# Half of the feed-forward's first product in four blocks by seven products for eight, with the second product's units moved to the odd blocks

## The chip, the cores and the metric

One core of a Trainium2 chip runs the whole kernel. The metric is the time on the device in microseconds (us); a lower one is better. TensorE (PE) multiplies matrices into PSUM, VectorE (DVE) and ScalarE (ACT) work element by element, GpSimd (POOL) issues some of the DMAs and SyncE (SP) the others.

## The reference, cut to what matters

The reference is a decoder trunk of two layers over 256 tokens of width 2048, all in float32. Each layer has an attention and then a feed-forward part; only the second is touched:

```python
FFN_HIDDEN = 5632

def _swiglu(h, w_in, w_out):
    g, u = jnp.split(h @ w_in, [FFN_HIDDEN], axis=-1)
    return (jax.nn.silu(g) * u) @ w_out

def reference(x, positions, norm_gains, ...):
    for i in range(DEPTH):
        ...
        x = x + _rmsnorm(y, g[1])
        y = _swiglu(_rmsnorm(x, g[2]), ffn_w_in[i], ffn_w_out[i])
        x = x + _rmsnorm(y, g[3])
    return x
```

`_rmsnorm` divides a token's row by its root mean square and multiplies by a gain for each column. The kernel puts the gains on the transposed tokens, and multiplies by the token's factor (`rstd`) only behind the first product, as a scale for each row.

## The kernel before, in words

**Split numbers.** A float32 matrix product is made of three passes in the reduced format fp32r. Each operand is split into a high part (ScalarE rounds it, line 104) and a low part (VectorE subtracts, line 105), and `mm3` (line 95) adds high x high, high x low and low x high in PSUM. So each piece of weights that is loaded costs two ScalarE casts and two VectorE subtractions of 128x1024 (`split_weight`, halves of the piece), and each use of it with 128 tokens costs 4 x 3 = 12 matmuls with 512 columns. Below, such a group of 12 is called a product. The split halves go to six buffers each (`whi`, `wlo`), which is room for three pieces.

**Blocks.** The 5632 hidden columns are handled in 11 blocks of 512 (`ffn`, line 458). `block_in` (line 463) makes a block's gate and up sums: for m = 0 (gate) and m = 1 (up), for four pieces pc of the 2048 rows (512 rows each) it loads and splits a piece of `win` and multiplies it with both halves of the tokens (t = 0, 1): 16 products in four PSUM buffers (`mm`). The `yield` behind each piece hands over to the caller, which puts other work there. At the end ScalarE makes the silu of the gate sums (line 485), VectorE multiplies it with the up sums (line 487), and TensorE transposes the hidden values (line 492).

**Units.** The second product (hidden x `wout`) is done for pairs of blocks: hidden values of two token halves and two blocks, times the weights of two blocks and two groups of 512 output columns. `unit` (line 555) does this with seven products in place of eight (Strassen's scheme in Winograd's form). The token operands are sums that `pair_operands` (line 503) makes in `first` and `second`, as the two blocks of a pair end: three VectorE operations at the end of the first block, eight at the end of the second. The weight sums are made in three raw buffers (`wr`): `t` starts as B11, then gets B12 by an accumulating DMA from GpSimd (line 571), B22 by a VectorE add (line 568), and B21 by another; `b22` gets B12 by a second accumulating DMA. Each product reads one of these, split anew, and `gather` (lines 579 to 584) adds its sum to `y`. Two of the sums stay in PSUM and are accumulated on.

```python
factor = ("t", "t", "t", "b22", "b22", "b21", "t")
prepare(0)
now = split(w["t"])
yield
for k, left in enumerate(("A11", "S1", "S2", "S4", "S3", "A12", "A22")):
```

**The loop.** From block 2 on, each block has one unit of the pair before beside its own 16 products: the first two column groups in the even block, the other two in the odd one. At each `yield` of `block_in` the loop takes one step of the unit, so a unit's product stands behind each input piece until the seven are done. Block 10 has no partner: its pair's last unit and two plain column groups run beside it.

**What sets the order.** The order in which the code issues work is a priority. A planner at build time puts each engine's instructions in order: of those whose inputs and buffers are ready by its own reckoning, the earliest in the code goes first. A buffer of a pool is given to whoever comes when one is free. The order that comes out is fixed, and on the chip each engine follows it and waits where an input isn't there.

The names that the change touches: `block_in`, `x_piece` (line 326), `unit` with `prepare`, `gather` and `product`, the loop over `blk`, and `x`, the residual stream in SBUF (16 KB a partition), which is not read from the middle of block 0 to the end of block 10.

## Time and profile before

| what | us |
|---|---|
| median of 3 runs | 2108.28 (2108.18 to 2108.62) |
| the profiled execution, its own time | 2108.73 |
| its span (first to last instruction) | 2107.0 |
| mean granted clock of TensorE, share of full speed | 0.995 |
| feed-forward loop of layer 0: block 2 to block 9, cut at the transposes | 500.46 to 1009.76 |
| the same in layer 1 | 1482.60 to 1991.01 |

The profile is of one execution. A line such as "L105" is a line of the kernel's source; "wlo<-w,whi" names the tile that is written and those that are read. Busy time of TensorE overlaps from matmul to matmul, since their ends are modelled: what one costs is seen from start to start. Idle time is put down to what ended it.

### The profile page before, as it was taken

To read this page: it belongs to the slowest core of one execution; us is meant where nothing else is said; L and a number is where in the kernel's file an instruction comes from. 1 tells how busy PE (TensorE), PEld (TensorE's weight loads), DVE (VectorE), ACT (ScalarE), POOL (GpSimd) and SP (SyncE) were. 2 spreads that over 40 slices of the span, in tenths; PEclk is the share of its full clock that TensorE was granted. 3 is DMA by queue.
4 is the path that set the end of the run, shared out by engine and by line. 5 is a ranking of instruction groups with operands and counts; after the bars stand their busy time and mean duration, and the time that the engine had idled before them with its cause. 6 is when DMAs were issued, how large, how long until landed. Compare 5 with 4: busy or idle time off the path is not lost.

```text
span 2107.0 us, 26201 instructions
## 1 busy us (share of the span) xinstructions
PE 2075.4 (98%) x10372; PEld 1770.4 (84%) x10372; DVE 1466.5 (70%) x1697; ACT 1100.6 (52%) x1427; POOL 74.3 (4%) x119
## 2 busy tenths in 40 slices
PE   8999999999999999999998999999999999999997
PEld 7999998788888888888888898878888888888886
DVE  6655555756767778777767776575768768778766
ACT  6444444544555545555445554454555555546543
POOL 0000000000000000000000100000000000000000
PEclk9999999999999999999999999999999999999999
DMA  7554556465676666676644533555566776666663
GB/s 266 200 173 167 163 178 229 153 217 154 226 240 206 206 187 228 220 250 203 198 163 159 209 121 137 182 216 181 197 194 212 239 240 201 213 185 222 217 200 105
DMA packets 62044, 413.85 MB, mean 196 GB/s; under 512 B 7392, under 2 KB 7648, under 8 KB 13920
## 3 DMA queue, kind: packets, MB, share of 16 engines
q1 hardware_dynamic: 56736, 374.42, 49.0%
q0 software_dynamic: 5184, 37.75, 9.8%
q8 instruction: 81, 1.33, 0.3%
q14 instruction: 43, 0.35, 0.0%
HBM read 410.05 MB, written 2.10 MB: 196 GB/s over the span
## 4 chain that ended last, share of the span: by engine, by line
PE 87%; issue 5%; DVE 4%; DMA 2%; ACT 1%; POOL 0%; SPq 0%; POOLq 0%; DVEq 0%; ACTq 0%
PE ps L99 23%; PE ps L101 23%; PE ps L100 23%; PE wp L100 5%; PE wp L101 4%; PE wp L99 4%; DMA wr<-in_wout 2%; DVE wlo L105 2%; DVE x L259 1%; PE pt L492 1%; PE pt L111 1%; PE ps_s L906 0%; PE ps_s L386 0%; PE ps_s L907 0%; PE po L425 0%
## 5 line engine op out<-in xcount | busy, mean ns | idle before, releaser
L105 DVE TENSOR_TENSOR wlo<-w,whi 128x1024 fp32r<-128x1024 f32 (+2 forms) x598 | 716.5, 1205 | 309.5 <-ACT whi L104 297.6
L104 ACT CAST whi<-w 128x1024 fp32r<-128x1024 f32 (+2 forms) x598 | 613.8, 1036 | 452.7 <-PE ps L101 248.5
L99 PE MATMUL ps<-whi,xTh 128*128 128x512 f32 (+2 forms) x1632 | 627.5, 389 | 3.0 <-ACT xTh L104 1.5
L100 PE MATMUL ps<-wlo,xTh 128*128 128x512 f32 (+2 forms) x1632 | 629.4, 387 | 0.0
L101 PE MATMUL ps<-whi,xTl 128*128 128x512 f32 (+2 forms) x1632 | 628.7, 387 | 0.4 <-DVE xTl L105 0.4
L105 DVE TENSOR_TENSOR wlo<-wr,whi 128x1024 fp32r<-128x1024 f32 x252 | 303.2, 1222 | 212.7 <-ACT whi L104 205.9
L104 ACT CAST whi<-wr 128x1024 fp32r<-128x1024 f32 x252 | 261.8, 1050 | 361.0 <-PE ps L101 241.1
L99 PEld LDWEIGHTS ps<-whi,xTh 128*128 128x128 f32 x1632 | 308.1, 189 | 63.9 <-ACT xTh L104 4.4
L101 PEld LDWEIGHTS ps<-whi,xTl 128*128 128x128 f32 x1632 | 307.9, 189 | 60.7 <-DVE xTl L105 0.6
L100 PEld LDWEIGHTS ps<-wlo,xTh 128*128 128x128 f32 x1632 | 308.1, 189 | 59.7 <-DVE wlo L105 0.4
L99 PE MATMUL ps<-xTh,whi 128*128 128x256 f32 x512 | 146.3, 287 | 0.0
L101 PE MATMUL ps<-xTh,wlo 128*128 128x256 f32 x512 | 144.9, 283 | 0.0
L100 PE MATMUL ps<-xTl,whi 128*128 128x256 f32 x512 | 144.7, 283 | 0.0
L99 PE MATMUL ps<-whi,oTh 128*128 128x512 f32 x256 | 100.7, 393 | 0.0
L100 PE MATMUL ps<-wlo,oTh 128*128 128x512 f32 x256 | 100.0, 391 | 0.0
L101 PE MATMUL ps<-whi,oTl 128*128 128x512 f32 x256 | 99.9, 390 | 0.0
L100 PEld LDWEIGHTS ps<-xTl,whi 128*128 128x128 f32 x512 | 98.2, 192 | 0.3
L99 PEld LDWEIGHTS ps<-xTh,whi 128*128 128x128 f32 x512 | 98.1, 192 | 0.3
L101 PEld LDWEIGHTS ps<-xTh,wlo 128*128 128x128 f32 x512 | 98.2, 192 | 0.2 <-DVE wlo L105 0.2
L584 DVE TENSOR_TENSOR y<-y,wp 128x512 f32<-128x512 f32 x110 | 74.9, 681 | 23.0 <-PE wp L101 23.0
L568 DVE TENSOR_TENSOR wr<-wr 128x2048 f32<-128x2048 f32 x36 | 82.2, 2283 | 0.0
L571 POOL DMA_DIRECT2D wr<-in_wout x36 | 31.3, 868 | 1215.3 <-DVE wlo L105 1215.3
(229 smaller groups left out, 2427.0 us busy)
## 6 DMA issues: line engine op xcount, KB each, us to landing
w<-in_win SPq DMA_DIRECT2D x176, 1024.0 KB, 5.3
wr<-in_wout SPq DMA_DIRECT2D x54, 1024.0 KB, 6.1
wr<-in_wout POOLq DMA_DIRECT2D x36, 1024.0 KB, 8.6
w<-in_wqk SPq DMA_DIRECT2D x32, 1024.0 KB, 4.9
w<-in_wo SPq DMA_DIRECT2D x32, 1024.0 KB, 4.9
w<-in_wout SPq DMA_DIRECT2D x16, 1024.0 KB, 5.0
w<-in_wv SPq DMA_DIRECT2D x15, 1024.0 KB, 4.9
w<-in_wdown SPq DMA_DIRECT2D x8, 724.0 KB, 4.8
```

The lines of the kernel that those rows point to most:

```text
L99: nc.tensor.matmul(out, lh, rh, start=first, stop=False, skip_group_check=more)
L100: nc.tensor.matmul(out, lh, rl, start=False, stop=False, skip_group_check=more)
L101: nc.tensor.matmul(out, ll, rh, start=False, stop=last, skip_group_check=more)
L104: nc.scalar.copy(hi, src)
L105: nc.vector.tensor_tensor(lo, src, hi.bitcast(F32), op=ALU.subtract)
L111: nc.tensor.transpose(pt[:, j * P : (j + 1) * P], src[:, j * P : (j + 1) * P], ident)
L259: nc.vector.scalar_tensor_tensor(xs, y[:, t, cg * CW : (cg + 1) * CW], ry, xs, op0=ALU.mult, op1=ALU.add)
L492: nc.tensor.transpose(pt[:, j * P : (j + 1) * P], hs[t][:, j * P : (j + 1) * P], ident)
L568: nc.vector.tensor_tensor(into, into, w, op=ALU.add)
L571: nc.gpsimd.dma_start(into, wout[blk, cg], accum_op=ALU.add)
L584: nc.vector.tensor_tensor(ys(t, cg), ys(t, cg), ps, op=op)
```

## The change

In blocks 2, 4, 6 and 8 `block_in_sevens` takes the place of `block_in`. Of the four pieces of 512 rows, the first two are done with seven products for eight: two token halves by two row pieces, times two row pieces by gate and up. The other two pieces are done plainly, eight products. Some of the seven sums are also needed apart, so they are copied to `G` (pool `gp`) by ScalarE, and VectorE combines them there while the sum in PSUM is accumulated on. The weight sums are made as in a unit, by `right_factors`, which both now share.

The scheme adds values of different tokens, which have different factors `rstd`. So the transposed second half of the tokens is multiplied by the ratio of the two factors and split again (`rescale`, during block 0), and from block 1 on the first half's factor serves both. The token operands are made once a layer (`input_operands`, behind block 1) and lie in the place of `x`, which is stored to DRAM in block 0 (`spill`) and loaded again behind block 8 (`x_again`).

The units of the second product now run in the odd blocks only, both of a pair in one block (`chained`): two products ahead of the block's first piece, then one or two in turn behind each piece. The seven products of a unit come in another order, A11, A12, S1, S4, S2, S3, A22, which changes when each weight sum is made and read. An even block of the four has no unit.

```diff
...
@@ -323,10 +324,11 @@
                 kc == 0, kc == KC - 1,
             )
 
-    def x_piece(ps, piece, kcs, t, n=None):
+    def x_piece(ps, piece, kcs, t, first=None, more=False):
+        first = kcs[0] == 0 if first is None else first
         for k, kc in enumerate(kcs):
             ts_ = slice(t * P, (t + 1) * P)
-            mm3(ps, (xTh[:, kc, ts_], xTl[:, kc, ts_]), piece[k], kc == 0, kc == KC - 1)
+            mm3(ps, (xTh[:, kc, ts_], xTl[:, kc, ts_]), piece[k], first and k == 0, kc == KC - 1, more)
 
     def diff_attention():
@@ -453,12 +455,31 @@
...
     PAIRS = [(b, b + 1) for b in range(0, NBLK - 1, 2)]
     def ffn(i, rstd, second_tokens, first_tokens, aside=None):
         win, wout = a[f"win{i}"], a[f"wout{i}"]
         y = ypool.tile([P, NT, D], F32, tag="y", name="y")
         ss = small.tile([P, NT, NCG], F32, tag="ss", name="ss")
+        rows = rstd
+        def activation(g, u, hidden):
+            hs = []
+            for t in range(NT):
+                sg = sb.tile([P, CW], F32, tag="t2k", bufs=4, name="sg")
+                nc.scalar.activation(sg, g(t), AF.Silu, scale=rows[t])
+                h = sb.tile([P, CW], F32, tag="t2k", bufs=4, name="h")
+                nc.vector.scalar_tensor_tensor(h, u(t), rows[t], sg, op0=ALU.mult, op1=ALU.mult)
+                hs.append(h)
+            for t in (1, 0):
+                pt = tr.tile([P, CW], F32, tag="tr", name="pt")
+                for j in range(4):
+                    nc.tensor.transpose(pt[:, j * P : (j + 1) * P], hs[t][:, j * P : (j + 1) * P], ident)
+                hidden(t, pt.rearrange("p (k t) -> p k t", k=4))
         def block_in(blk, hidden):
             ps = {}
@@ -471,26 +492,124 @@
                     if blk or m:
                         for t in range(NT):
                             x_piece(ps[m, t], pieces[-1], range(pc * 4, pc * 4 + 4), t)
-                        yield
+                        if not blk:
+                            rescale(pc)
+                    yield
                 if not (blk or m):
                     for t in range(NT):
                         if t == 1:
                             second_tokens()
                         for pc in range(4):
                             x_piece(ps[m, t], pieces[pc], range(pc * 4, pc * 4 + 4), t)
+                    spill()
             yield
...
+            activation(lambda t: ps[0, t], lambda t: ps[1, t], hidden)
+        I = {}
+        def spill():
+            I["x"] = dram.tile([P, NT, D], F32, name="x_kept")
+            nc.gpsimd.dma_start(I["x"], x)
+            inv = small.tile([P, 1], F32, tag="r", name="inv")
+            nc.vector.reciprocal(inv, rstd[0])
+            c = small.tile([P, 1], F32, tag="r", name="c")
+            nc.vector.tensor_tensor(c, rstd[1], inv, op=ALU.mult)
+            full = sb.tile([P, P], F32, tag="t2k", bufs=4, name="full")
+            nc.vector.tensor_scalar(full, ident, 0.0, c, op0=ALU.mult, op1=ALU.add)
+            pt = tr.tile([P, CW], F32, tag="tr", name="ptc")
+            nc.tensor.transpose(pt[:, :P], full, ident)
+            I["c"] = gp.tile([P, CW], F32, tag="g", name="ratio")
+            nc.scalar.copy(I["c"][:, :P], pt[:, :P])
+            I["raw"] = wr.tile([P, 4, 4, P], F32, tag="r", name="raw")
+        def whole(out, ks, ts_):
+            nc.vector.tensor_tensor(out, xTh[:, ks, ts_].bitcast(F32), xTl[:, ks, ts_].bitcast(F32), op=ALU.add)
+        def rescale(cg):
+            ks, ts_ = slice(cg * 4, cg * 4 + 4), slice(P, SEQ)
+            if cg < 2:
+                out = I["raw"][:, cg]
+            else:
+                out = sb.tile([P, 4, P], F32, tag="t2k", bufs=4, name="xs")
+            whole(out, ks, ts_)
+            nc.vector.tensor_tensor(out, out, I["c"][:, :P].unsqueeze(1).broadcast_to([P, 4, P]), op=ALU.mult)
+            split_to(xTh[:, ks, ts_], xTl[:, ks, ts_], out)
+        def input_operands():
+            s = xpool.tile([P, 4, 2, 4, P], F32R, tag="x", name="S")
+            a21, a22, a11, a12 = (I["raw"][:, j] for j in range(4))
+            def put(j, src):
+                split_to(s[:, j, 0], s[:, j, 1], src)
+                return s[:, j, 0], s[:, j, 1]
+            def col(k, t):
+                ks, ts_ = slice(k * 4, k * 4 + 4), slice(t * P, (t + 1) * P)
+                return xTh[:, ks, ts_], xTl[:, ks, ts_]
+            for k in range(2):
+                whole(I["raw"][:, 2 + k], slice(k * 4, k * 4 + 4), slice(0, P))
+                for t in range(NT):
+                    I[f"A{t + 1}{k + 1}"] = col(k, t)
+            nc.vector.tensor_tensor(a22, a21, a22, op=ALU.subtract)
+            I["-S1"] = put(0, a22)
+            nc.vector.tensor_tensor(a22, a22, a11, op=ALU.subtract)
+            I["S2"] = put(1, a22)
+            nc.vector.tensor_tensor(a21, a11, a21, op=ALU.subtract)
+            I["S3"] = put(2, a21)
+            nc.vector.tensor_tensor(a12, a12, a22, op=ALU.add)
+            I["-S4"] = put(3, a12)
+        def block_in_sevens(blk, hidden):
+            ps = {k: mm.tile([P, CW], F32, tag="mm", name="ps") for k in ((0, 1), (1, 0), (1, 1), (0, 0))}
+            G = {k: gp.tile([P, CW], F32, tag="g", name="G") for k in ("11", "12", "22")}
+            lone = wp.tile([P, CW], F32, tag="wp", name="lone")
+            begun = set()
+            def plain(m, pc, t, piece=None):
+                piece = load_split(win[blk, m, pc], [4, CW]) if piece is None else piece
+                x_piece(ps[m, t], piece, range(pc * 4, pc * 4 + 4), t, (m, t) not in begun, True)
+                begun.add((m, t))
+                return piece
+            right = right_factors(win[blk, 0, 0], win[blk, 1, 0], win[blk, 0, 1], win[blk, 1, 1])
+            def step(k, left, out, key=None):
+                product(out, I[left], right(k), more=key in begun or k in (4, 5))
+                if key:
+                    begun.add(key)
+            a, c = ps[0, 1], ps[1, 0]
+            right(None)
+            yield
+            step(0, "A11", a, (0, 1))
+            nc.scalar.copy(G["11"], a)
+            u2 = plain(1, 2, 0)
+            plain(1, 2, 1, u2)
+            step(1, "A12", ps[0, 0], (0, 0))
+            step(2, "-S1", lone)
+            nc.scalar.copy(G["22"], lone)
+            u3 = plain(1, 3, 0)
+            plain(1, 3, 1, u3)
+            step(3, "-S4", c, (1, 0))
+            step(4, "S2", a)
+            nc.vector.tensor_tensor(G["12"], G["22"], a, op=ALU.subtract)
+            nc.vector.tensor_tensor(G["12"], c, G["12"], op=ALU.add)
+            g2 = plain(0, 2, 0)
+            step(5, "S3", a)
+            nc.vector.tensor_tensor(G["22"], G["22"], a, op=ALU.subtract)
+            nc.vector.tensor_tensor(G["22"], ps[1, 1], G["22"], op=ALU.add)
+            g3 = plain(0, 3, 0)
+            nc.vector.tensor_tensor(G["11"], ps[0, 0], G["11"], op=ALU.add)
+            plain(0, 2, 1, g2)
+            step(6, "A22", a, (0, 1))
+            plain(0, 3, 1, g3)
+            yield
+            activation(lambda t: a if t else G["11"], lambda t: G["22"] if t else G["12"], hidden)
         def parts(name):
             both = mid.tile([P, 2, 2, 4, P], F32R, tag="mid", name=name)
@@ -552,23 +671,36 @@
             for k in range(4):
                 mm3(ps, (lhs[0][:, k], lhs[1][:, k]), rhs[k], not more and k == 0, k == 3, more)
 
+        def right_factors(b11, b12, b21, b22):
+            w = {}
+            def raw(src):
+                t = wr.tile([P, 4, CW], F32, tag="r", name="wr")
+                nc.sync.dma_start(t, src)
+                return t
+            def right(k):
+                if k is None:
+                    w["t"] = raw(b11)
+                    w["b21"] = raw(b21)
+                    return
+                now = split_weight(w[("t", "b21", "t", "b22", "t", "b22", "t")[k]], [4, CW])
+                if k == 0:
+                    nc.gpsimd.dma_start(w["t"], b12, accum_op=ALU.add)
+                    w["b22"] = raw(b22)
+                elif k == 3:
+                    nc.vector.tensor_tensor(w["t"], w["t"], w["b22"], op=ALU.add)
+                    nc.gpsimd.dma_start(w["b22"], b12, accum_op=ALU.add)
+                elif k == 4:
+                    nc.vector.tensor_tensor(w["t"], w["t"], w["b21"], op=ALU.add)
+                return now
+            return right
         def unit(pair, X, cgs, first):
             (b1, b2), (n1, n2) = pair, cgs
-
...
             def sums():
                 return wp.tile([P, CW], F32, tag="wp", name="wp")
@@ -583,52 +715,43 @@
                     op = ALU.add if sign > 0 else ALU.subtract
                     nc.vector.tensor_tensor(ys(t, cg), ys(t, cg), ps, op=op)
 
...
-            factor = ("t", "t", "t", "b22", "b22", "b21", "t")
-            prepare(0)
-            now = split(w["t"])
+            right = right_factors(wout[b1, n1], wout[b1, n2], wout[b2, n1], wout[b2, n2])
+            right(None)
             yield
-            for k, left in enumerate(("A11", "S1", "S2", "S4", "S3", "A12", "A22")):
-                if k:
-                    now = split(w[factor[k]])
-                if k < 6:
-                    prepare(k + 1)
+            for k, left in enumerate(("A11", "A12", "S1", "S4", "S2", "S3", "A22")):
                 if k == 0:
                     pa = sums()
-                elif k in (1, 5):
+                elif k in (1, 2):
                     pc = sums()
-                ps, more = (pc, k == 3) if k in (1, 3, 5) else (pa, k > 0)
-                product(ps, X[left], now, more)
+                ps, more = (pc, k == 3) if k in (1, 2, 3) else (pa, k > 0)
+                product(ps, X[left], right(k), more)
                 if k == 0:
                     gather(0, n1, ps, 1.0, first)
                 elif k == 1:
+                    gather(0, n1, ps, 1.0)
+                elif k == 2:
                     gather(1, n2, ps, -1.0, first)
-                elif k == 2:
+                elif k == 3:
                     gather(0, n2, ps, -1.0, first)
-                elif k == 3:
+                elif k == 4:
                     gather(0, n2, ps, -1.0)
-                elif k == 4:
+                elif k == 5:
                     gather(1, n2, ps, -1.0)
-                elif k == 5:
-                    gather(0, n1, ps, 1.0)
                 else:
                     gather(1, n1, ps, 1.0, first)
+                yield
+        def chained(units):
+            one, two = units
+            next(one)
+            yield
+            for k in range(7):
+                if k == 6:
+                    next(two)
+                next(one)
+                yield
+            for _ in two:
                 yield
         def plain_unit(pair, X, cgs):
@@ -661,6 +784,11 @@
             for _ in steps:
                 pass
 
+        def x_again():
+            nonlocal x
+            x = xpool.tile([P, NT, D], F32, tag="x", name="x")
+            nc.gpsimd.dma_start(x, I["x"])
         steps = plain = iter(())
         pair = X = None
         for blk in range(NBLK):
@@ -672,14 +800,23 @@
                 X, hidden, second = pair_operands(blk == NBLK - 3)
             else:
                 hidden = second
+            sevens = 1 < blk < NBLK - 1 and blk % 2 == 0
             if blk > 1 and blk % 2 == 1:
-                steps = unit(*before, (2, 3), blk == 3)
+                steps = chained([unit(*before, cgs, blk == 3) for cgs in ((0, 1), (2, 3))])
+            elif blk == NBLK - 1:
+                steps = unit(pair, X, (0, 1), False)
+            next(steps, None)
+            if blk > 1 and blk % 2 == 1:
                 next(steps)
-            elif blk > 1:
-                steps = unit(*((pair, X) if blk == NBLK - 1 else before), (0, 1), blk == 2)
                 next(steps)
-            for n, _ in enumerate(block_in(blk, hidden)):
-                if blk < NBLK - 1 or n not in (4, 5):
+            for n, _ in enumerate((block_in_sevens if sevens else block_in)(blk, hidden)):
+                if sevens:
+                    continue
+                if blk < NBLK - 1:
+                    next(steps, None)
+                    if n % 2 == 1:
+                        next(steps, None)
+                elif n not in (4, 5):
                     next(steps, None)
                 if n % 2 == 1:
                     next(plain, None)
@@ -690,6 +827,12 @@
                     if blk == NBLK - 1:
                         ahead = load_split(wout[blk, 0], [4, CW])
             drain(steps)
+            if blk == 1:
+                input_operands()
+            if blk == NBLK - 3:
+                x_again()
+            if blk == 0:
+                rows = {t: rstd[0] for t in range(NT)}
             if blk == 2 and aside is not None:
                 aside()
             if blk % 2 == 1:
```

## Rows read from the trace of the kernel before

**Rows 1.** The page's first part: busy us, share, instructions.
```profile
PE 2075.4 (98%) x10372; PEld 1770.4 (84%) x10372; DVE 1466.5 (70%) x1697; ACT 1100.6 (52%) x1427; POOL 74.3 (4%) x119
```

**Rows 2.** The page's chain of waits that ended last, share by engine.
```profile
PE 87%; issue 5%; DVE 4%; DMA 2%; ACT 1%; POOL 0%; SPq 0%; POOLq 0%; DVEq 0%; ACTq 0%
```

**Rows 3.** Windows of blocks, a pair, a stretch; columns in the first line.
```profile
core 0: us, PE busy (x) PEld busy (x) DVE busy (x) ACT busy (x) POOL busy (x), PEclk, DMA share, GB/s
500.46:563.92 63.46, 63.46 (x286) 52.63 (x285) 46.76 (x46) 36.02 (x42) 1.71 (x2) 1.00 0.65 216
627.38:692.40 65.02, 64.02 (x286) 52.55 (x285) 49.82 (x50) 34.74 (x38) 1.71 (x2) 1.00 0.64 210
692.40:819.37 126.97, 126.97 (x569) 105.18 (x568) 96.43 (x94) 68.49 (x74) 3.47 (x4) 1.00 0.66 215
755.33:776.00 20.67, 20.67 (x97) 17.20 (x96) 20.67 (x22) 13.40 (x16) 0.00 (x0) 1.00 0.37 131
```

**Rows 4.** Timeline of TensorE, blocks 5 and 6: start, length, what, idle before.
```profile
700.78 0.39 PE L99 MATMUL wp<-whi,S_S 128*128 128x512 f32 x1
...
703.50 0.39 PE L99 MATMUL ps<-whi,xTh 128*128 128x512 f32 x1
...
755.86 1.04 PE L492 MATMUL pt<-ident,h 128*128 128x128 f32 x8
756.65 0.48 PE L99 MATMUL wp<-whi,A_S 128*128 128x512 f32 x1
```

**Rows 5.** Timeline of GpSimd and ScalarE in block 4.
```profile
649.28 0.86 POOL L571 DMA_DIRECT2D wr<-in_wout  x1 [32.45 <-DVE wlo L105]
...
659.52 1.99 ACT L104 CAST whi<-wr 128x1024 fp32r<-128x1024 f32 x2 [8.60 <-DMA wr<-in_wout]
```

**Rows 6.** Timeline of TensorE at the same place.
```profile
660.01 0.39 PE L101 MATMUL ps<-whi,xTl 128*128 128x512 f32 x1
660.63 0.49 PE L99 MATMUL wp<-whi,A_S 128*128 128x512 f32 x1 [0.23 <-ACT whi L104]
661.89 0.50 PE L100 MATMUL wp<-wlo,A_S 128*128 128x512 f32 x1 [0.77 <-DVE wlo L105]
```

**Rows 7.** Timeline of VectorE in blocks 5 and 6.
```profile
723.50 2.36 DVE L105 TENSOR_TENSOR wlo<-wr,whi 128x1024 fp32r<-128x1024 f32 x2 [8.95 <-ACT whi L104]
...
760.04 2.28 DVE L568 TENSOR_TENSOR wr<-wr 128x2048 f32<-128x2048 f32 x1
762.24 0.69 DVE L105 TENSOR_TENSOR S_S<-h,S_S 128x512 fp32r<-128x512 f32 x1
762.84 0.68 DVE L584 TENSOR_TENSOR y<-y,wp 128x512 f32<-128x512 f32 x1
763.44 2.35 DVE L105 TENSOR_TENSOR wlo<-w,whi 128x1024 fp32r<-128x1024 f32 x2
```

**Rows 8.** Groups by line and shape: count, busy us, mean ns, idle before.
```profile
L105 DVE TENSOR_TENSOR wlo<-w,whi 128x1024 fp32r<-128x1024 f32 x570 | 692.1, 1221 | 296.8 <-ACT whi L104 285.4
L568 DVE TENSOR_TENSOR wr<-wr 128x2048 f32<-128x2048 f32 x36 | 82.2, 2283 | 0.0
L584 DVE TENSOR_TENSOR y<-y,wp 128x512 f32<-128x512 f32 x110 | 74.9, 681 | 23.0 <-PE wp L101 23.0
L487 DVE SCALAR_TENSOR_TENSOR h<-ps,rs,sg 128x512 f32<-128x512 f32 x44 | 32.9, 748 | 2.2 <-PE ps L101 1.6
```

**Rows 9.** Waits: who for whom, us in total, times, longest.
```profile
ACT whi L104 <- DMA wr<-in_wout: 106.8, 18, 8.6
```

**Rows 10.** The page's DMA issues: count, KB each, median us to landing.
```profile
wr<-in_wout POOLq DMA_DIRECT2D x36, 1024.0 KB, 8.6
```

**Rows 11.** Timeline of TensorE within a unit's product in block 6.
```profile
790.12 0.40 PE L99 MATMUL wp<-whi,A_S 128*128 128x512 f32 x1
790.35 0.62 PE L99 MATMUL ps<-whi,xTh 128*128 128x512 f32 x2
```

**Rows 12.** Window of blocks 0 and 1, layer 0; columns as above.
```profile
424.00:500.46 76.46, 76.46 (x343) 63.31 (x342) 39.43 (x36) 36.65 (x39) 1.04 (x1) 1.00 0.62 201
```

More of the change, by code (lines that the diff above doesn't have):

```diff
@@ L53, in trunk_kernel @@
     tr = ctx.enter_context(tc.tile_pool(name="tr", bufs=2, space=PSUM))
+    dram = ctx.enter_context(tc.tile_pool(name="dram", bufs=2, space=bass.MemoryType.DRAM))
     mm = sba = wst = wr = wp = None
@@ L489, in block_in @@
-            for t in (1, 0):
-                pt = tr.tile([P, CW], F32, tag="tr", name="pt")
-                for j in range(4):
-                    nc.tensor.transpose(pt[:, j * P : (j + 1) * P], hs[t][:, j * P : (j + 1) * P], ident)
-                hidden(t, pt.rearrange("p (k t) -> p k t", k=4))
+            activation(lambda t: ps[0, t], lambda t: ps[1, t], hidden)
[14 more added lines that the diff above has]
+            I["raw"] = wr.tile([P, 4, 4, P], F32, tag="r", name="raw")
```

31 lines of the change are left out of this document (removed).

## The prediction

> **What bounds the kernel now.** I read the busy table first: TensorE is busy for 98% of the span, VectorE for 70%, ScalarE for 52% [rows 1]. The chain of waits says the same: 87% of it is TensorE, and VectorE's 4% and the 2% on accumulating loads are the rest that matters here [rows 2]. Then the table by stage, cut at the transposes that end a feed-forward block. A block takes 63.46 us with TensorE busy throughout and the clock at 1.00. A pair of blocks takes 126.97 us with VectorE at 96.43 and ScalarE at 68.49 [rows 3]. In the timeline twelve matmuls, one product of 128 tokens by 512 rows by 512 columns, go from 700.78 to 703.50: 2.72 us, 0.227 each [rows 4]. A block holds 23 products: 23 x 2.72 + 0.9 for eight transposes (755.86 to 756.65, [rows 4]) = 63.5. So TensorE has nothing to give but work, and what decides is whether the others still feed it.
>
> They nearly failed already. At 649.28 GpSimd issues an accumulating load; ScalarE sits behind it, 8.60 us idle, until 659.52, and TensorE loses 1.5 us at 660.01 to 662 [rows 5, 6]. That block is the one of 65.02 [rows 3].
>
> **The change, part by part.**
>
> *Removed on TensorE.* Four blocks in each of two layers do 15 products for 16: 8 x 12 matmuls x 0.227 = 21.8 us, all on the path. Added there: one small transpose a layer, 0.2 for both. The moved units are the same number of products.
>
> *Added on VectorE.* I charge it start to start, not by duration: two splits of 128x1024 end 2.35 us after the first starts, so one takes 1.13 and the last 1.22; the 128x2048 add is followed after 2.20, a 128x512 operation after 0.60 [rows 7]; the durations stand in [rows 8]. A split weight piece is two subtractions, 2.27. A changed block has 11 pieces for 8, two 2.20 adds and five 0.60 operations that combine sums: 6.8 + 4.4 + 3.0 = 14.2 more per pair. 96.4 + 14.2 = 110.6 of 126.97 - 2.72 = 124.25: 89%. ScalarE goes from 68.5 to 76 (six casts of 1.0 [rows 5] and two copies of half that size more). Neither is the bound on average.
>
> *The spread.* The odd blocks now hold two units. VectorE there: 44 subtractions 50.0, four adds 8.8, 14 gathers 8.4, two gate multiplies 1.5, eight operations on the operands of the second block 4.8: 73.5, against 30 x 2.72 + 0.9 = 82.6. No stall of its own. The tight stretch begins where the odd block's last input piece ends, 5.44 us (two unit products) ahead of the changed block, and ends where that block's seventh product starts, 13 products in: 5.44 + 35.4 = 40.8 us. VectorE must do in it 11 pieces 25.0, adds 4.4, combinations 3.0, gates 1.5, operands 4.8, gathers 1.2: 39.9. It fits with 0.9 to spare if it never idles; before, it ran from 755.33 to 776.00, in the same place, without a gap, and TensorE lost nothing [rows 3, 7]. I charge 0.2 in the six such blocks that follow an odd block with units, 1.2 in all (bounds 0 and what full durations give, below).
>
> The Trainium skill bears on this. Its page "VectorE: DVE Perf Modes", section "The DRAIN you can't avoid", says that the next operation cannot issue until the pipe of the one before is empty. The pair of 2.35 where two durations make 2.44 disagrees. By the rule the rival "no change" below would be the forecast.
>
> *Accumulating loads.* 36 become 52. ScalarE waits for one 18 times, 106.8 us in all, 5.9 each [rows 9]; landing takes 8.6 [rows 10]. Before, the load into the second raw buffer is issued when step 3 is split and is wanted by step 4, one product and one input piece later: 8.16 us on TensorE, and rows 6 show this to be the edge. The first load of a unit, wanted at the next step before, is now wanted two steps later, with 10.9 us between: safe. The second is now also wanted two steps later. In the odd blocks that is 10.9 and 16.3 us, but it first waits for a 2.20 add: as good as before. In a changed block it is steps 3, 4 and one plain product, 8.16 us, less the add: 2.2 us short. What can cover that is the other gate piece's first product, 2.72, which needs neither; then the loss is nil. I take the middle, 1.1 x 8 = 8.8 (bounds 0 and 17.6). Queued behind the waiting cast on ScalarE are the next casts, and VectorE waits for those.
>
> *Sums read between accumulations.* In a changed block one sum is read after step 4 and again after step 5 and then written again, with one product (2.72) between; VectorE needs 0.68 plus at most the 2.28 of the add it may be in: 2.96. In the odd blocks two unit products stand back to back on one sum. The order is planned with readiness known, and TensorE slips single matmuls of another product in where one is not ready (790.35, [rows 11]). I charge nothing; without that cover it would be 0.2 a block there and up to 2.3 at each of 16 places.
>
> *Block 0, block 1 and x.* Rescaling the second tokens (12 operations), the seven-product operands (10) and three small ones are 25 x 0.60 = 15 us of VectorE a layer at most. Blocks 0 and 1 have no unit in either kernel, and VectorE is busy 39.43 of 76.46 there [rows 12]: hidden in 37 idle us. Without that cover, 30 us in all. Storing x, 2 MB on GpSimd's queue, has nothing behind it. Loading it again has: it is issued after the last use of the operands in block 8, four products (10.9 us) ahead of block 9, whose first accumulating load stands behind it. A 1 MB load on that queue lands in 8.6, so 17.2 at most [rows 10]: up to 6.3 late. I take 1 a layer, 2.0 (bounds 0 and 12.6).
>
> **The sum.** -21.8 + 0.2 + 1.2 + 8.8 + 2.0 = -9.6. The profiled execution took 2108.73 (span 2107.0): 2099.1. The median of the runs is 0.45 lower, so I predict 2099.
>
> **The rivals.**
>
> *Everything is hidden.* All stalls at nothing: 2108.7 - 21.6 = 2087. For it: VectorE at 89%, TensorE without a gap in nearly all blocks now. Against: the stretch at 98% and the shorter cover of the load.
>
> *No change.* If each VectorE operation cost its full duration, the tight stretch would hold [rows 8] 22 x 1.22 + 4.6 + 3.4 + 1.5 + 5.4 + 1.4 = 43.1, 2.3 over 40.8. Eight times 2.3 = 18; 2108.7 - 21.6 + 18 = 2105. The same comes of the loads at their upper bound, 17.6. For it: VectorE also waits for casts, as at 723.50 [rows 7]. Against: the pitch in rows 7.
>
> *Slower: ScalarE parked behind accumulating loads.* In-order ScalarE stops for a load that is planned too early, and with it VectorE, idle 8.95 at 723.50 [rows 7]. VectorE has 124.25 - 110.6 = 13.6 us free per pair. If each of the three second loads of a pair costs it 5.9 as now, it needs 110.6 + 17.7 = 128.3: 1.3 more than the pair took before, 11 us over eight: 2119. It decides from 5.5 us each. For it: 18 such waits now, one a unit. Against: the loads are wanted a step later than before.
>
> The Trainium skill's page "DMA: Bandwidth & Descriptors", section "Anatomy of one DMA — SWDGE (gpsimd) path", fits such a load as 2.0 us plus its bytes over 436 GB/s. For 1 MB I estimate 4.4 us from it. With that this rival and the 8.8 of the sum would go; the 8.6 of rows 10 decides.
>
> **How the numbers follow.** Forecast (2093 to 2104) 0.46; all hidden (below 2093) 0.22; no change (2104 to 2112.5) 0.18; slower 0.14. 0.2%, 4.2 us, is about what can be told from no change. So faster 0.68, same 0.18, slower 0.14. The range runs from all hidden, 2086, to 2114: it leaves out most of the slower rival.
>
> **What would show it.** Matmul records fall by 94 (96 less, two more). Pairs in the loop of 124.3 to 126 us say that the saving came through; 127 or more that it was eaten. Idle ScalarE ahead of a cast in the even blocks, ended by the accumulating load, with TensorE's gap a few us later, confirms the 8.8; gaps at the start of the even blocks with VectorE gapless say the burst; VectorE below 105 per pair says that I counted it wrong. A gap early in block 9 would be the load of x. I am wrong if TensorE's gaps in the even blocks sum to over 2 us each, or if stretches outside the loop move by more than 2 us.

## The result, and the profile after

The changed kernel takes 2125.5 us (2125.1 to 2126.8), the kernel before 2108.5 beside it: ratio 1.0078 [1.0061, 1.0096], slower by 17 us where I had forecast 9 less. The profiled execution has a span of 2123.6, 16.6 more than before.

The busy table (us, share, count) says that the work came out as counted: 10278 matmuls, 94 fewer than in [rows 1].

```profile
PE 2066.8 (97%) x10278; PEld 1756.8 (83%) x10278; DVE 1606.5 (76%) x1851; ACT 1160.7 (55%) x1509; POOL 90.3 (4%) x139
```

The chain of waits names what grew. TensorE's share falls from 87% [rows 2] to 75%; DVE goes from 4 to 9 and DMA from 2 to 8.

```profile
PE 75%; DVE 9%; DMA 8%; issue 6%; ACT 2%; POOL 0%; SPq 0%; ACTq 0%; POOLq 0%; DVEq 0%
```

The windows of the first three pairs of blocks in layer 0, cut as in [rows 3] (columns as there):

```profile
546.02:672.67 126.65, 124.79 (x558) 102.94 (x556) 107.16 (x99) 78.37 (x89) 5.12 (x6) 1.00 0.74 222
672.67:802.77 130.10, 126.54 (x557) 103.92 (x556) 110.51 (x106) 75.00 (x81) 5.17 (x6) 0.99 0.71 218
802.77:932.27 129.50, 126.68 (x557) 104.06 (x556) 111.15 (x107) 75.17 (x81) 5.72 (x7) 0.99 0.77 236
```

A pair holds 12 matmuls fewer, and the last two of these take 130.1 and 129.5 where a pair took 127.0. Their 110.5 and 111.2 of VectorE are the 110.6 that I had counted, ScalarE's 75 the 76. So nothing costs more work than foreseen; TensorE stands still in between. I measured its loss as the start-to-start time of successive matmuls over 0.227, summed by block. In the two loops it is 39.7 us, 32.7 of them in the eight changed blocks and 7.0 in the odd ones; before it was 3.6. With -21.8 for the matmuls: -21.8 + 39.7 - 3.6 = +14.3 of the 16.6.

**One stall, followed through block 6.** GpSimd's timeline (start, length, what, idle before) shows both accumulating loads of that block, the second issued at 769.57:

```profile
747.99 0.85 POOL L690 DMA_DIRECT2D wr<-in_win  x1 [21.16 <-DVE wlo L106]
769.57 0.85 POOL L694 DMA_DIRECT2D wr<-in_win  x1 [20.73 <-DVE wlo L106]
```

ScalarE's timeline: its next cast is the one that wants the load (`wr`), and it waits 6.25 us. The cast of a plain gate piece (`w`), whose product I had named as the cover, stands behind it.

```profile
770.27 1.05 ACT L105 CAST whi<-w 128x1024 fp32r<-128x1024 f32 x1 [0.32 <-PE ps L102]
777.57 1.99 ACT L105 CAST whi<-wr 128x1024 fp32r<-128x1024 f32 x2 [6.25 <-DMA wr<-in_win]
779.47 1.99 ACT L105 CAST whi<-w 128x1024 fp32r<-128x1024 f32 x2
```

VectorE's timeline: the load waits for the last subtractions that read its buffer, which stand behind the add L693 and end the group of four at 766.81. The combination of sums (L600) comes only behind the two subtractions of the late piece.

```profile
764.01 2.28 DVE L693 TENSOR_TENSOR wr<-wr 128x2048 f32<-128x2048 f32 x1
766.81 4.62 DVE L106 TENSOR_TENSOR wlo<-wr,whi 128x1024 fp32r<-128x1024 f32 x4
...
774.69 1.22 DVE L106 TENSOR_TENSOR wlo<-w,whi 128x1024 fp32r<-128x1024 f32 x1
778.65 2.36 DVE L106 TENSOR_TENSOR wlo<-wr,whi 128x1024 fp32r<-128x1024 f32 x2 [2.74 <-ACT whi L105]
780.92 0.68 DVE L600 TENSOR_TENSOR G<-G,ps 128x512 f32<-128x512 f32 x1
```

TensorE's timeline: step 3's product starts at 770.02. TensorE stands from 778.2 to 780.6 for the cast of the plain piece (`xTh` is the operand of a plain product, `S` that of one of the seven), and again until 781.7 for L600, since the next product writes the sum that L600 reads. The matmuls after that start 0.43 apart, not 0.227:

```profile
770.02 0.62 PE L100 MATMUL ps<-whi,S 128*128 128x512 f32 x2
...
777.95 0.39 PE L102 MATMUL ps<-whi,xTl 128*128 128x512 f32 x1
780.56 0.49 PE L100 MATMUL ps<-whi,xTh 128*128 128x512 f32 x1 [2.22 <-ACT whi L105]
781.66 0.80 PE L100 MATMUL ps<-whi,S 128*128 128x512 f32 x1 [0.61 <-DVE G L600]
782.25 0.63 PE L101 MATMUL ps<-wlo,S 128*128 128x512 f32 x1
782.68 0.63 PE L102 MATMUL ps<-whi,S 128*128 128x512 f32 x1
...
785.05 0.39 PE L102 MATMUL ps<-whi,S 128*128 128x512 f32 x1
```

The windows of this place show why (PEclk is the third column from the end): the granted clock is near its lower level, 1.2 GHz, for three microseconds.

```profile
777.00:782.00 5.00, 2.17 (x8) 1.29 (x8) 3.35 (x4) 3.89 (x4) 0.00 (x0) 0.94 0.97 400
782.00:785.00 3.00, 3.00 (x8) 2.32 (x8) 2.48 (x3) 0.38 (x1) 0.00 (x0) 0.53 0.92 333
785.00:790.00 5.00, 5.00 (x23) 4.10 (x23) 4.15 (x5) 1.73 (x2) 0.00 (x0) 1.00 0.71 239
```

Block 6 so loses 2.4 + 0.9 + 1.5, and little else. The same chain stands in six of the eight changed blocks, all but the two blocks 2: the waits for the cast are 1.4 to 3.4, 14.6 in all, those for L600 0.87 each, 5.2, and the half clock, which comes four times in the loops, makes some 7 of the 39.7.

In the whole execution the waits (who for whom; us, times, longest) are 140.0 us of ScalarE behind loads into raw buffers, against 106.8 of the one row of [rows 9], and now they reach TensorE:

```profile
ACT whi L105 <- DMA wr<-in_wout: 80.4, 17, 7.5
ACT whi L105 <- DMA wr<-in_win: 59.6, 13, 7.3
PE ps L100 <- ACT whi L105: 16.6, 9, 3.2
```

### The profile page after: what moved, and what is told of

It reads as the page before. It is cut to its first block, busy times and chain, and to the rows that moved or that the text cites. A ratio compares the mean times of both kernels' runs of the same rounds, so it can differ in the third digit from the quotient of the medians.

```text
span 2123.6 us, 26407 instructions
## 1 busy us (share of the span) xinstructions
PE 2066.8 (97%) x10278; PEld 1756.8 (83%) x10278; DVE 1606.5 (76%) x1851; ACT 1160.7 (55%) x1509; POOL 90.3 (4%) x139
## 4 chain that ended last, share of the span: by engine, by line
PE 75%; DVE 9%; DMA 8%; issue 6%; ACT 2%; POOL 0%; SPq 0%; ACTq 0%; POOLq 0%; DVEq 0%
PE ps L100 20%; PE ps L101 20%; PE ps L102 20%; DVE wlo L106 5%; DMA wr<-in_win 5%; PE wp L102 4%; PE wp L101 4%; PE wp L100 4%; DMA wr<-in_wout 2%; ACT whi L105 2%; DVE wr L693 1%; DVE x L260 1%; PE ps_s L1049 0%; PE ps_s L388 0%; PE ps_s L1050 0%
## 5 line engine op out<-in xcount | busy, mean ns | idle before, releaser
L106 DVE TENSOR_TENSOR wlo<-w,whi 128x1024 fp32r<-128x1024 f32 (+3 forms) x534 | 637.7, 1203 | 253.6 <-ACT whi L105 244.4
L105 ACT CAST whi<-w 128x1024 fp32r<-128x1024 f32 (+3 forms) x534 | 546.7, 1034 | 441.6 <-PE ps L102 255.9
L100 PE MATMUL ps<-whi,xTh 128*128 128x512 f32 (+2 forms) x1472 | 566.4, 391 | 19.9 <-ACT whi L105 16.6
L101 PE MATMUL ps<-wlo,xTh 128*128 128x512 f32 (+2 forms) x1472 | 570.0, 388 | 3.5 <-DVE wlo L106 3.4
L102 PE MATMUL ps<-whi,xTl 128*128 128x512 f32 (+2 forms) x1472 | 566.8, 387 | 1.4 <-DVE xTl L106 1.4
L106 DVE TENSOR_TENSOR wlo<-wr,whi 128x1024 fp32r<-128x1024 f32 x364 | 436.1, 1219 | 155.6 <-ACT whi L105 152.8
L105 ACT CAST whi<-wr 128x1024 fp32r<-128x1024 f32 x364 | 374.8, 1049 | 311.7 <-PE ps L102 107.2
L100 PEld LDWEIGHTS ps<-whi,xTh 128*128 128x128 f32 x1472 | 277.5, 189 | 78.3 <-ACT whi L105 20.5
L101 PEld LDWEIGHTS ps<-wlo,xTh 128*128 128x128 f32 x1472 | 278.1, 189 | 59.0 <-DVE wlo L106 6.5
L696 DVE TENSOR_TENSOR wr<-wr 128x2048 f32<-128x2048 f32 x26 | 59.4, 2285 | 0.3
L693 DVE TENSOR_TENSOR wr<-wr 128x2048 f32<-128x2048 f32 x26 | 59.4, 2284 | 0.1
```

Source lines behind the costliest of these rows:

```text
L100: nc.tensor.matmul(out, lh, rh, start=first, stop=False, skip_group_check=more)
L101: nc.tensor.matmul(out, lh, rl, start=False, stop=False, skip_group_check=more)
L102: nc.tensor.matmul(out, ll, rh, start=False, stop=last, skip_group_check=more)
L105: nc.scalar.copy(hi, src)
L106: nc.vector.tensor_tensor(lo, src, hi.bitcast(F32), op=ALU.subtract)
L693: nc.vector.tensor_tensor(w["t"], w["t"], w["b22"], op=ALU.add)
```

## The experiments

Theory T1 is that chain: the second accumulating load (`b22` gets B12) lands late in a changed block, ScalarE's order parks behind it, TensorE runs dry and its clock falls. The rival T2 is that VectorE has no room in the changed blocks. "Loss" is the loss above, for the changed blocks in order, layer 0 | layer 1, but counting only gaps over 0.13 us, which leaves out some 0.2 a block; by this count the changed kernel's are 1.8, 2.3, 4.8, 4.9 | 1.8, 3.4, 5.0, 7.2, 31.2 in all. Ratios are to the kernel before on the same chip. Each kernel is planned anew, so orders elsewhere may shift a little as well.

**e1: no second load in the changed blocks** (`second` is a new argument of `right_factors`, False from `block_in_sevens`).

```diff
+                    if second:
                         nc.gpsimd.dma_start(w["b22"], b12, accum_op=ALU.add)
```

> Leaves out the addition of B12 to the b22 buffer (the second accumulating load) in the four changed blocks of each layer; all else as in the changed kernel. The theory (ScalarE parks behind this load, the combining operations on VectorE queue behind it, and TensorE runs dry): the even blocks' loss on TensorE, 32.7 us in the changed kernel, falls under 10, no stretch at half clock stays in the loop, and the time is 2096 to 2102 (2125.5 less some 25). The rival (VectorE has no room in the even blocks, whatever it waits for): the load is only where the lack shows, the loss moves elsewhere, 2118 to 2125.

Measured 2102.0, 0.9968 [0.9955, 0.9980]: 23.5 less. Loss 0.7, 0.9, 1.2, 1.2 | 0.7, 1.0, 1.3, 2.5, 9.5 in all (11.7 where the changed kernel has the 32.7, a little over the 10 expected). T1 holds. TensorE doesn't fall to half clock in the loops; the window around block 6 has it at 1.00 throughout:

```profile
750.00:800.00 50.00, 49.15 (x219) 40.09 (x218) 42.97 (x44) 30.19 (x32) 0.86 (x1) 1.00 0.61 199
```

**e2: no second load anywhere, units included** (both lines above removed).

> Leaves out the same addition in the units too. The theory: the odd blocks' 7 us go as well, 2088 to 2095, near the 2087 at which everything is hidden. The rival (VectorE without room): 2115 to 2125, little from the run with the even blocks alone.

Measured 2098.8, 0.9950 [0.9935, 0.9965], 4 above the expected range. By the medians the units' second loads cost about 3 us in all, though the intervals of e1 and e2 overlap. The changed blocks still lose 0.7 to 2.0 each, for another reason.

**e3: the second load kept, the last VectorE add left out in the changed blocks** (`last` is False there).

```diff
-                elif k == 4:
+                elif k == 4 and last:
                     nc.vector.tensor_tensor(w["t"], w["t"], w["b21"], op=ALU.add)
```

> Leaves out VectorE's last add of weights (t plus B21, 2.20 us) in the four changed blocks; it comes after the second accumulating load is issued, so that load and its wait stay as they are. The theory: that add runs while VectorE would wait anyway, within 5 us of the changed kernel, 2120 to 2126. The rival (VectorE without room): 8 x 2.2 = 17.6 us less, 2106 to 2110.

Measured 2129.4, 1.0095 [1.0080, 1.0110]: no gain at all from 2.2 us of VectorE a block. T2 as the main cause falls. T1's range is missed by 3; the intervals of this and the changed kernel overlap.

**e4: the units moved and reordered, no sevens, no storing of x.**

```diff
-            sevens = 1 < blk < NBLK - 1 and blk % 2 == 0
+            sevens = False
-                        if not blk:
-                            rescale(pc)
-                    spill()
-            if blk == 1:
-                input_operands()
-            if blk == NBLK - 3:
-                x_again()
-            if blk == 0:
-                rows = {t: rstd[0] for t in range(NT)}
```

> The moved units and their new order alone: every block does its first product with 16 plain products, x is neither stored nor rescaled. The theory: the even blocks lose nothing, the odd ones some 3 to 7 us at the second load of their first unit, 2109 to 2115. The rival (two units in one block leave VectorE late, and the even block after it pays): the even blocks still lose 2 us and more each, 2122 to 2130.

Measured 2106.1, 0.9984 [0.9975, 0.9994], below my range. No block of the loops loses anything, and the stall of block 4 before [rows 5, 6] is gone too, which is most of the 3 us. The moved units are free, and even 3 us better than where they were.

**f1 and f2: issue the second load earlier.** In f1 the add `t += b22` goes from step 3 to step 2 and the load stays. In f2 step 3 goes ahead of step 2 in the changed blocks, and add and load follow the later of the two splits, step 2's:

```diff
             step(1, "A12", ps[0, 0], (0, 0))
+            step(3, "-S4", c, (1, 0))
             step(2, "-S1", lone)
...
-            step(3, "-S4", c, (1, 0))
...
-                elif k == 3:
+                elif k == at:
                     nc.vector.tensor_tensor(w["t"], w["t"], w["b22"], op=ALU.add)
```

> As the changed kernel, but the add of B22 to t (2.20 us of VectorE) stands behind step 2's split in place of step 3's, in changed blocks and units, so that the second accumulating load need not wait for it and is issued some 2.2 us earlier. The theory (the load is late by the 2 to 4 us that TensorE waits): 8 x 2 us and the half-clock stretches go, 2105 to 2113. The rival (what counts is where the waiting cast stands in ScalarE's order, not when the load is issued): within 5 us of the changed kernel, 2120 to 2127.

> As the changed kernel, but in the changed blocks step 3 stands ahead of step 2, and the add and the second accumulating load follow step 2's split: between that split and step 5 are four products and a piece more (13.6 us on TensorE, 8.2 before). The theory: as if the load were not there, 2099 to 2106, faster than the kernel before. The rival (the waiting cast's place counts): 2115 to 2127.

f1: 2121.7, 1.0062 [1.0045, 1.0079], 4 less and not the 12 and more I expected, and its interval overlaps the changed kernel's. In block 6 the edit changes nothing: VectorE does the add ahead of the four subtractions in either kernel, and the load, which waits for them, is issued at 769.75. So f1 doesn't tell what an earlier issue is worth. f2 (`at` is 2 in the changed blocks): 2142.2, 1.0155 [1.0140, 1.0170], a plain miss. GpSimd's and ScalarE's timelines in block 6 of f2: the load is issued at 773.94, no earlier, since the add that it waits for comes late on VectorE, and with a plain 1 MB load issued 0.5 us behind it it takes 11.1 us:

```profile
773.94 0.85 POOL L694 DMA_DIRECT2D wr<-in_win  x1 [17.91 <-DVE wr L693]
...
776.74 1.05 ACT L105 CAST whi<-w 128x1024 fp32r<-128x1024 f32 x1
785.14 1.99 ACT L105 CAST whi<-wr 128x1024 fp32r<-128x1024 f32 x2 [7.36 <-DMA wr<-in_win]
```

An earlier place in the code is not an earlier issue while VectorE, which must add first, is behind.

**f3: f2 with x loaded a block later** (`if blk == NBLK - 2: x_again()`).

> The same, and x is loaded again behind block 9, not behind block 8. The theory that the load of x delays block 9's first accumulating load: 2 to 3 us less than the run with x loaded behind block 8. The rival (block 9's loss of 1.1 to 1.5 us in each layer has another cause): within 1 us of it.

Measured 2140.0, 1.0146 [1.0131, 1.0161]; block 9 loses 1.1 and 1.2 as in f2. The load of x isn't what costs there.

**f4: a plain load and a VectorE add in place of the accumulating load in the changed blocks.**

```diff
-                    nc.gpsimd.dma_start(w["b22"], b12, accum_op=ALU.add)
+                    again = wst.tile([P, 4, CW], F32, tag="w", name="again")
+                    nc.sync.dma_start(again, b12)
+                    nc.vector.tensor_tensor(w["b22"], w["b22"], again, op=ALU.add)
```

> As the changed kernel, but in the changed blocks b22 gets B12 by a plain load into a buffer of the pool wst and a VectorE add of 2.20 us. The load waits for nothing that VectorE does, so nobody is parked behind it. The theory (the second load is late because VectorE lets it start late and it then takes 8 to 11 us): near the run without that load, 2101 to 2110. The rival (VectorE has no room): 8 x 2.2 us more VectorE work in the tight blocks, 2122 to 2142.

Measured 2109.0, 1.0005 [0.9996, 1.0013]: 16 us come back, though VectorE has 2.2 us a block more to do. That speaks against T2 more strongly than e3. The plain load moves the same 1 MB, so it isn't the bytes as such either. Loss 0.9 to 3.0.

**f7: a second copy of B22, accumulated on at once, two steps earlier** (step 5 splits `s`, and the load into `b22` goes, in the changed blocks).

```diff
+                elif k == 1 and not second:
+                    w["s"] = wst.tile([P, 4, CW], F32, tag="w", name="s")
+                    nc.sync.dma_start(w["s"], b22)
+                    nc.gpsimd.dma_start(w["s"], b12, accum_op=ALU.add)
```

> As the changed kernel, but in the changed blocks B22 is loaded a second time, into a buffer of wst, at step 1, and B12 is accumulated on that copy at once; step 5 reads it. No VectorE work is added, and the accumulating load waits for no split. The theory: 2100 to 2108. The rival (an accumulating load is late wherever it is issued, because ScalarE's order counts on a shorter one): ScalarE is still idle ahead of step 5's cast and the time is 2115 or more. What could spoil it: only one wst buffer is left for the plain pieces meanwhile.

Measured 2151.3, 1.0198 [1.0184, 1.0212], a miss. The casts of `s` no longer wait, but now two accumulating loads run together and both are slow, 11.8 and 15.0 us to landing: by GpSimd's and ScalarE's timelines the first factor's, issued at 759.29, is there 15 us later, and with one plain staging buffer left a plain piece is 9.5 late.

```profile
755.68 0.85 POOL L695 DMA_DIRECT2D s<-in_win  x1 [17.54 <-DMA wr<-in_win]
759.29 0.85 POOL L690 DMA_DIRECT2D wr<-in_win  x1 [2.76 <-DVE wlo L106]
...
774.35 1.99 ACT L105 CAST whi<-wr 128x1024 fp32r<-128x1024 f32 x2 [8.90 <-DMA wr<-in_win]
...
800.09 2.00 ACT L105 CAST whi<-w 128x1024 fp32r<-128x1024 f32 x2 [9.50 <-DMA w<-in_win]
```

**f8: a quarter of the second load, at the same place** (`w["b22"][:, :1]`, `b12[:, :1]` in the changed blocks).

> As the changed kernel, but the second accumulating load of the changed blocks adds only a quarter of B12 (256 KB of 1 MB), issued at the same place. If the time goes with how long the load takes, it lands sooner, ScalarE's wait shrinks from 6 to 3 us or less, and the time is 2103 to 2113. If it is the issue that is late, or VectorE that has no room, the time stays at 2118 to 2126.

Measured 2103.3, 0.9973 [0.9962, 0.9985], near e1. The load is there, issued behind the same split, and the cast needs it; only its landing is short. It is the landing time that costs. The DMA issues of this kernel (count, KB each, median us to landing):

```profile
wr<-in_win POOLq DMA_DIRECT2D x8, 1024.0 KB, 8.7
wr<-in_win POOLq DMA_DIRECT2D x8, 256.0 KB, 3.8
```

**f10 and f9: all second loads in two halves, without and with f1's earlier add.**

```diff
-                    nc.gpsimd.dma_start(w["b22"], b12, accum_op=ALU.add)
+                    for h in (slice(0, 2), slice(2, 4)):
+                        nc.gpsimd.dma_start(w["b22"][:, h], b12[:, h], accum_op=ALU.add)
```

> The two halves alone, the add where it was. The theory: between the changed kernel and the run with both, 2106 to 2116. The rival: 2120 to 2128.

> As the changed kernel, but the second accumulating load goes in two halves (512 KB each), the first of which the first cast of the piece reads, and the add of B22 to t stands behind step 2's split. The theory (time goes with how late the piece's bytes are): 2.2 us from the add and 2 to 4 from the first half's landing, which is most of the 2.9 us that a changed block loses to the load: 2100 to 2110. The rival (landing times grow when two loads share the queue, so nothing is won): 2118 to 2126.

f10: 2110.7, 1.0012 [1.0003, 1.0021]; f9: 2111.2, 1.0009 [1.0000, 1.0018]. The halves give back some 15 us with the same bytes: a cast of 128x1024 needs one half only, and they land in a median 6.8 us, two at once. The earlier add gives nothing more.

**g1 and g2: what is left in e1.** g1 also leaves out both VectorE adds on `t` in the changed blocks; g2 leaves out the read of sum `a` behind step 5 in place of that:

```diff
             step(5, "S3", a)
-            nc.vector.tensor_tensor(G["22"], G["22"], a, op=ALU.subtract)
```

> As the run without the second load in the changed blocks (2102), and there without both VectorE adds of weights as well: 4.4 us of VectorE a block less. If VectorE's room is what is still lost: the wait for the low part of a piece goes, 0.3 to 1.8 us a block, 2094 to 2098. If it is the read between the accumulations: 2100 to 2103.

> As the run without the second load in the changed blocks (2102), and there without the VectorE operation that reads the sum after step 5 (G22 minus a), before step 6's accumulation: TensorE need not wait for it. If the read between accumulations is what is still lost: the 0.66 us in each of eight blocks goes, 2095 to 2098. If it is VectorE's room: 2100 to 2103.

g1: 2097.7, 0.9950 [0.9934, 0.9965]; loss 0.7 in each of the eight blocks. g2: 2096.2, 0.9942 [0.9929, 0.9956]; loss 0, 0.3, 0.3, 0.6 | 0, 0.4, 0.7, 1.5. Each takes a part of its own. TensorE's waits name them: first e1, then g1, then g2 (us, times, longest).

```profile
PE ps L101 <- DVE wlo L106: 5.1, 8, 1.7
PE ps L100 <- DVE G L604: 4.0, 8, 0.5
```
```profile
PE ps L101 <- DVE wlo L106: 2.8, 3, 1.4
PE ps L100 <- DVE G L604: 4.0, 8, 0.5
```
```profile
PE ps L101 <- DVE wlo L106: 5.7, 10, 1.4
```

L604 is the read of `a`. Its wait is 0.5 as listed and 0.66 start to start, eight times: 5.3. The adds' lateness on VectorE is the other part: 4.3 by the medians of e1 and g1, whose intervals overlap a little.

**g3: half of the second load accumulated, half loaded plainly and added by VectorE, in the changed blocks.**

```diff
+                        nc.gpsimd.dma_start(w["b22"][:, 2:], b12[:, 2:], accum_op=ALU.add)
+                        again = wst.tile([P, 4, CW], F32, tag="w", name="again")
+                        nc.sync.dma_start(again[:, :2], b12[:, :2])
+                        nc.vector.tensor_tensor(w["b22"][:, :2], w["b22"][:, :2], again[:, :2], op=ALU.add)
```

> As the changed kernel, with the whole sum: in the changed blocks one half of B12 comes to b22 by a plain load and a VectorE add of half the size, the other by an accumulating load of 512 KB. The theory: both are there by 5 to 6 us, for half the VectorE work of the plain load and add alone (2109): 2103 to 2109. The rival (each way's cost adds up): 2110 to 2120.

Measured 2105.2, 0.9986 [0.9977, 0.9995]: the whole computation, 20 us below the changed kernel and 3 below the one before. That, like e4's gain, is within the 0.2% that I had named as the limit, though the intervals stop short of 1. Loss 0.9 to 2.3.

## Why the prediction was wrong, step by step

**The step that failed: "Accumulating loads ... I take the middle, 1.1 x 8 = 8.8 (bounds 0 and 17.6)".** Taking these loads out of the changed blocks gives 23.5 us (e1), 2.9 a block, above my upper bound. The wait for the cast alone, 14.6 in six blocks, lies within the bounds; what goes beyond them is what queued behind it, L600's 5.2 and the half clock's 7. (With the loads gone some 4 of that come back, as waits for L604.) Two things were missing, the cover and the clock; the lead was about right:

- The cover. I named "the other gate piece's first product, 2.72, which needs neither". It doesn't need the load, but its casts stand behind the waiting cast in ScalarE's fixed order, and L600 stands behind the late subtractions on VectorE: the cover is parked with what it was to cover. Before, ScalarE and TensorE had already stopped for one load [rows 5, 6]; I read those rows for the length of the wait and not for what is queued behind it.
- The lead. I counted 8.16 us from step 3's split to step 5, less the add: 2.2 short of the edge of [rows 5, 6]. In block 6 the add L693 does stand ahead of the subtractions, in a stretch that VectorE works through without a gap from 758.3 to 775.9. The split is done at 769.57, when TensorE is about to start step 3. Step 5's place on TensorE is 8.6 us later, at 778.2, where the load of [rows 5, 6] had 10.9: 2.3 short, and the waits for the cast are 2.4 on average. The load lands at 777.5, ahead of that place; the cast, the subtractions and L600 behind it are not. In the two blocks 2, which follow no odd block with units, the load is issued 3.4 us ahead of step 3's product, ScalarE waits for it all the same (3.3 and 3.6), and TensorE loses 1.1 and 1.2 behind it in place of 2.3 to 7.2. In the other six it is issued between 0.8 us ahead of that product and 0.9 behind. The timelines of GpSimd, TensorE and ScalarE in block 2 of layer 0:

```profile
512.60 0.85 POOL L694 DMA_DIRECT2D wr<-in_win  x1 [23.61 <-DVE wlo L106]
516.05 0.39 PE L100 MATMUL ps<-whi,S 128*128 128x512 f32 x1
520.93 2.00 ACT L105 CAST whi<-wr 128x1024 fp32r<-128x1024 f32 x2 [3.29 <-DMA wr<-in_win]
```

- The clock. I gave no price to what follows a wait: some 7 us at half clock.

The Trainium skill's page "DMA: Bandwidth & Descriptors", section "Anatomy of one DMA — SWDGE (gpsimd) path", whose estimate of 4.4 us I set aside for the measured 8.6, is not borne out for accumulating loads: 256 KB take 3.8 (f8), 512 KB 5.4 (in g3), 1 MB 8.3 to 8.8. Through the first and the last, 0.75 MB in 4.9 us, these are 2.1 us plus the bytes at 160 GB/s. So the Trainium skill's fixed part of 2.0 agrees and its rate of 436 GB/s does not, here.

**"Sums read between accumulations. I charge nothing".** Wrong too. In the changed kernel TensorE waits for the read behind step 4 (L600) in the six blocks above and for the one behind step 5 (L604) in the two blocks 2, 0.66 each. Once the loads are gone, L604 costs 0.66 in all eight blocks, 5.3 (e1; g2 gets back 5.8), three times the 0.2 a block that I gave as the price without cover. Of the product that I had put in between, the planner placed seven of the twelve matmuls ahead of step 5, so five, 1.1 us, were left. TensorE's timeline in block 6 of e1:

```profile
780.14 0.39 PE L102 MATMUL ps<-whi,S 128*128 128x512 f32 x1
780.37 0.39 PE L101 MATMUL ps<-wlo,xTh 128*128 128x512 f32 x1
...
781.28 0.39 PE L102 MATMUL ps<-whi,xTl 128*128 128x512 f32 x1
782.17 0.50 PE L100 MATMUL ps<-whi,xTh 128*128 128x512 f32 x1 [0.50 <-DVE G L604]
```

**The tight stretch, 1.2.** The mechanism was there and the term too small: 4.3 by e1 and g1. "It fits with 0.9 to spare" forgot that VectorE also waits for ScalarE in it.

**The load of x, 2.0.** Not shown: block 9's loss doesn't change when it comes later (f3). That was tried on f2 only. In the changed kernel, too, block 9's loss of 1.1 in each layer stands 26 us into the block, behind a unit's second load, and not early in it.

**What was right.** The 96 matmuls at 0.227: with the loads and then the adds, or the reads, taken away the time falls to 2098 and 2096, toward the 2087 of "everything is hidden". As a ledger, of the second loads and then of one thing each from e1: 2108.5 - 21.6 + 23.5 (second loads, changed blocks) + 3.2 (units' second loads, e2) + 5.3 (reads) + 4.3 (adds) = 2123.2 of 2125.5. That is closer than it should be: it leaves out the 3 us that the moved units save by themselves (e4). With them it comes to about 2120, and 5 to 6 us stay unexplained; e2's and g1's terms are no larger than their intervals, and all of them taken away together was not run. The moved units cost nothing (e4). VectorE's sum was exact, and it works at the pitch that I took, not at full durations, so "no change" by that way falls. (Its price was also too high by its own rule: I charge the stretch in six blocks, and took eight there; 6 x 2.3 would have been 14, not 18.)

**The rivals.** "Slower: ScalarE parked behind accumulating loads" was the right one, with a chance of 0.14. That its 2119 is only 6 off is luck, since its price went by the wrong sum: it let VectorE's free time per pair absorb the waits, and decide "from 5.5 us each". The waits for `win` loads are 59.6/13 = 4.6 on average, VectorE has 19 us free in a pair of 130, and the kernel is slower all the same. A late piece stops TensorE at its own place, whatever is free elsewhere. The signs that I had named did show: two of the three pairs above over 127, gaps in the changed blocks behind ScalarE's wait, over 2 us a block in six of the eight.

## What to carry to other kernels

When a load is wanted later, ask not only whether it lands in time but what is queued behind the instruction that waits for it, on that engine and on the next: in a fixed order, independent work behind it is no cover. Slack averaged over a stage doesn't say whether the one piece is in time. A transfer can be cut (in halves, or half on another engine, f10 and g3) where it can't be issued earlier.

## What the runs showed of the hardware that I had not expected

- An accumulating 1 MB load into SBUF takes about 8.7 us, 11.1 with a plain 1 MB load issued 0.5 us behind it (f2), and 11.8 and 15.0 when two run together (f7). Windows of the changed kernel, behind the issue at 769.57 and before the next plain load at 774.80 (the last two columns are DMA share and GB/s): nothing moves for 1.4 us, and then this load alone keeps the DMA engines busy at 172 GB/s. In the window 777 to 782 above, nearly all of it plain loads, they moved 400 at 0.97.

```profile
769.60:771.00 1.40, 1.40 (x8) 1.17 (x7) 1.40 (x2) 1.08 (x2) 0.82 (x1) 1.00 0.00 0
771.00:774.80 3.80, 3.80 (x19) 3.14 (x18) 3.80 (x4) 0.32 (x1) 0.00 (x0) 1.00 0.99 172
```

- TensorE's granted clock fell to half four times in the loops, for about 3.4 us and once for 6.8, each time when TensorE had stood in two waits with one matmul between them (2.4 and 0.9 in block 6, 2.3 and 0.9 in block 8 of layer 0). The length of the waits alone doesn't decide it: in block 4 of layer 1 waits of 2.5 and 0.9 left it at full, as the starts 0.23 apart behind them in TensorE's timeline show. What does decide stays open here.

```profile
1639.82 0.39 PE L102 MATMUL ps<-whi,xTl 128*128 128x512 f32 x1
1642.55 0.50 PE L100 MATMUL ps<-whi,xTh 128*128 128x512 f32 x1 [2.35 <-ACT whi L105]
1643.65 0.50 PE L100 MATMUL ps<-whi,S 128*128 128x512 f32 x1 [0.60 <-DVE G L600]
1643.99 0.39 PE L101 MATMUL ps<-wlo,S 128*128 128x512 f32 x1
1644.22 0.39 PE L102 MATMUL ps<-whi,S 128*128 128x512 f32 x1
```
